# A hybrid decoder layer on one core: feed-forward expansions for all 1024 tokens by seven block products, down products as phases of their own, mixers between them

## The chip, the core and the metric

One core of a Trainium2 chip runs the kernel. The metric is the device time of one execution in microseconds (us). Engines are named as in the profile: PE is TensorE, which multiplies; PEld is its load of the stationary operand; DVE is VectorE, ACT is ScalarE, POOL is GpSimd, SP is SyncE, which here only issues DMAs. Each engine works through a queue of its own, in the order in which the built program holds it.

## What is computed

One decoder layer on x of 1024 tokens by 1024 channels, in float32:

```
x = x + 0.5 * swiglu(rms_norm(x, g1), wg1, wu1, wd1)        # D_FF = 2816
h = rms_norm(x, g2);  q, k, v, qi, ki, wi, u = split(h @ w_in)
score = sum over 4 heads of wi * relu(qi . ki), causal       # indexer
attn  = softmax attention, 8 heads x 64, each query over its 256 best-scored keys
pooled = multiscale_pool(u) @ pool_w * pool_scale
x = x + concat(attn, pooled) @ w_out
x = x + 0.5 * swiglu(rms_norm(x, g3), wg2, wu2, wd2)
swiglu(x, wg, wu, wd) = (silu(x @ wg) * (x @ wu)) @ wd
```

## The kernel before

**Arithmetic.** Every large operand is kept as a sum of two parts, `hi` and `lo`. `mm3` (lines 64 to 67) makes each 128-deep product from three matmuls: hi times hi, hi times lo, lo times hi. Weights come from HBM whole; `weight` (lines 161 to 174) loads a block of 128 x 512 into a buffer `r` (or `br` for the mixers), ACT casts it to the hi part (line 171) and DVE or POOL subtracts to get the lo part (line 172).

**Feed-forward.** `ffn` takes one half of the tokens (512) at a time. For each of 22 blocks of 128 hidden columns it makes the gate and the up product, 8 blocks of depth each (`expand`), and `act` (lines 198 to 205) makes the activation in SBUF. Four such blocks form a group; `down` multiplies a group into the residual, and each partial sum is added from its PSUM bank by DVE (line 220). The four banks' worth of accumulators are named `fg`, and only the feed-forward uses them.

**Mixer.** `mixer(h)` does one half: norm, indexer projection with rotary tables, indexer scores, pooling mixer, projections of v, k and q, then `top_masks`, `attention` and `out_proj`. `top_masks` finds each query's 256th best score bit by bit: 31 steps, each a count on ACT (line 445, Sign with an accumulator) and one on DVE (line 429) of the scores above a trial threshold, followed by four small instructions on DVE (lines 444, 448, 450, 451). A step needs the one before. Two blocks of 128 queries go in one run of 31 steps; half 0 has one run, half 1 has two. Mixers use the banks `ba`, `bt` and `pv` and weight buffers `br`, `bw` of their own.

**Order.** The program is written in the order ffn(0), mixer(0), ffn(1), mixer(1), second ffn(0), second ffn(1). A scheduler at build time then moves instructions within each engine's queue, in so far as buffers and data allow; splits and evacuations of the feed-forward carry a high priority. Since the feed-forward of one half needs nothing from the mixer of the other half, and has buffers of its own, its matmuls stand among those of the mixers.

Of the kernel before, what the change touches and what calls it, by code (L numbers as in the profile page):

```python
# [32 lines left out]
HIGH = 10_000_000  # L33


@with_exitstack
def hybrid_layer(ctx: ExitStack, tc: tile.TileContext, x, ffn1_norm, ffn1_w_gate, ffn1_w_up,
# [23 lines left out]
    def mm(o, lhs, rhs, start, stop):  # L61
        nc.tensor.matmul(o, lhs, rhs, start=start, stop=stop)  # L62
# [26 lines left out]
    x_dr = [dr.tile([HALF, D], F32, name=f"x_dr{h}") for h in range(2)]  # L89

# [9 lines left out]
    def load_x(h):  # L100
        new_x(h)
        for i in range(4):
            r0 = h * HALF + i * 128
            nc.sync.dma_start(x_at(h, i), x[0, r0:r0 + 128, :])
# [32 lines left out]
    def norm_transposed(h, which, region):  # L137
        hT = [t(f"X{region}{j}", [128, 4, HALF], F32R) for j in range(4)]
        xn = []
        for i in range(4):  # L140
            xi = t("sc", [128, D])
            ss = t("st", [128, 8])
            nc.scalar.activation(xi, x_at(h, i), AF.Square, accum_out=ss[:, :1])
            r = rstd_of(ss[:, :1], 1, D)
            nc.vector.tensor_scalar(xi, x_at(h, i), r[:, :1], None, op0=ALU.mult)
            xn.append(xi)
        for k in range(NK):
            ps = bank(("ba", "bt")[k % 2])
# [9 lines left out]
    nsplit = [0]  # L158
    alone = [True]

    def weight(src, tags=("r", "w")):
        """Both parts of a block of weights, [128, 2, a, b] for a source [128, a, b] of at most 512 columns."""
        _, a, b = src.shape
        n = a * b
        nsplit[0] += 1
        raw = t(tags[0], [128, 512])
        nc.sync.dma_start(raw[:, :n].rearrange("p (a b) -> p a b", a=a), src)
        w = t(tags[1], [128, 2, 512], F32R)
        eng = nc.vector if alone[0] or nsplit[0] % 3 == 0 else nc.gpsimd
        with tc.high_priority(offset=HIGH):  # L170
            nc.scalar.copy(w[:, 0, :n], raw[:, :n])  # L171
            eng.tensor_sub(w[:, 1, :n], raw[:, :n], f(w[:, 0, :n]))  # L172
        return w[:, :, :n].rearrange("p l (a b) -> p l a b", a=a)
# [4 lines left out]
    MIX = ("br", "bw")  # L178

# [1 line left out]
    def ffn(h, hT, wg, wu, wd, f0, f1, done=None):  # L181
        hi, lo = hT
        groups = []
        i = f0
        while i < f1:
            n = 4 if f1 - i >= 4 else 2
            groups.append(range(i, i + n))
            i += n
        def expand(ff, w):
            ps = bank("fg")  # L190
            for k0 in range(0, NK, 4):
                wt = weight(rows(w, k0, k0 + 4, ff * 128, (ff + 1) * 128))
                for k in range(k0, k0 + 4):
                    mm3(ps, wt[:, 0, k - k0], wt[:, 1, k - k0], hi[k], lo[k], k == 0, k == NK - 1)
            return ps

        def act(pg, pu):
            with tc.high_priority(offset=HIGH):
                s = t("t", [128, 512])
                nc.scalar.activation(s, pg, AF.Silu)  # L200
                nc.vector.tensor_mul(s, s, pu)  # L201
                a = t("a", [128, 2, 512], F32R)
                nc.scalar.copy(a[:, 0], s)  # L203
                (nc.vector if alone[0] else nc.gpsimd).tensor_sub(a[:, 1], s, f(a[:, 0]))  # L204
            return a

        def down(gr, acts):
            n = len(gr)
            for c in range(2):
                cols = slice(c * 512, (c + 1) * 512)  # L210
                wts = [weight(rows(wd, k, k + 1, c * 512, (c + 1) * 512)) for k in gr]
                for i in range(4):
                    ps = bank("fg")
                    tok = slice(i * 128, (i + 1) * 128)
                    for j in range(n):
                        mm3(ps, acts[j][:, 0, tok], acts[j][:, 1, tok], wts[j][:, 0, 0], wts[j][:, 1, 0],
                            j == 0, j == n - 1)
                    xo = x_at(h, i)[:, cols]
                    with tc.high_priority(offset=HIGH):
                        nc.vector.scalar_tensor_tensor(xo, ps, 0.5, xo, op0=ALU.mult, op1=ALU.add)  # L220
                    if done is not None and gr[-1] == NF - 1:
                        r0 = h * HALF + i * 128
                        nc.sync.dma_start(done[0, r0:r0 + 128, cols], xo)

        pend = None
        for gr in groups:
            acts = []
            for ff in gr:
                pg = expand(ff, wg)
                if pend is not None:  # L230
                    down(*pend)
                    pend = None
                acts.append(act(pg, expand(ff, wu)))
            pend = (gr, acts)
        down(*pend)

# [1 line left out]
    def out_proj(h, region):  # L238
        fetch_x(h)
        mt = [None] * 4  # L240
        for j in (2, 3, 0, 1):
            mt[j] = t(f"X{region}{j}", [128, 2, 2, HALF], F32R)
            nc.gpsimd.dma_start(mt[j].rearrange("p k l c -> p k (l c)"),
                                m_dr[h][2 * j:2 * j + 2].rearrange("k p l c -> p k (l c)"))
        for c in range(2):
            banks = [bank(n) for n in ("ba", "ba", "bt", "bt")]
            for n, k in enumerate((4, 5, 6, 7, 0, 1, 2, 3)):
                wt = weight(rows(w_out, k, k + 1, c * 512, (c + 1) * 512), MIX)
                m = mt[k // 2][:, k % 2]
                for i in range(4):  # L250
                    tok = slice(i * 128, (i + 1) * 128)
                    mm3(banks[i], m[:, 0, tok], m[:, 1, tok], wt[:, 0, 0], wt[:, 1, 0], n == 0, n == NK - 1)
# [5 lines left out]
    def proj(hT, c0, n):  # L258
        hi, lo = hT
        banks = [bank(n) for n in ("ba", "ba", "bt", "bt")]  # L260
        for k in range(NK):
            wt = weight(rows(w_in, k, k + 1, c0, c0 + n), MIX)
            for i in range(4):
                tok = slice(i * 128, (i + 1) * 128)
                mm3(banks[i][:, :n], hi[k][:, tok], lo[k][:, tok], wt[:, 0, 0], wt[:, 1, 0], k == 0, k == NK - 1)
        return banks

    def rope_tables(h):
        cs = t("cs", [128, 4, 2, HD])
# [3 lines left out]
    def index_proj(h, hT, cs):  # L273
        banks = proj(hT, C_I, N_I)
        for i in range(4):
# [18 lines left out]
            ps = bank("pv")  # L294
# [12 lines left out]
    def qk_proj(h, hT, cs, which):  # L307
        banks = proj(hT, (C_Q, C_K)[which], 512)
        for i in range(4):
# [17 lines left out]
            pt = bank("pv")  # L327
# [12 lines left out]
    def v_proj(h, hT):  # L340
        banks = proj(hT, C_V, 512)
# [7 lines left out]
    def pool_mixer(h, hT):  # L349
        hi, lo = hT  # L350
        tiles = []
        for g in range(4):
            ps = bank("bt")
            for kk in range(2):
                wt = weight(rows(w_in, 4 * kk, 4 * kk + 4, C_U + g * 128, C_U + (g + 1) * 128), MIX)
# [7 lines left out]
            po = bank("pv")  # L363
# [29 lines left out]
    def scores(h, i, sc):  # L393
        g = 4 * h + i
        n2 = (g // 2 + 1) * 256
        qi = t("qm", [128, 4, 256], F32R)
        for l in range(2):
            nc.gpsimd.dma_start(qi[l * 64:(l + 1) * 64], qi_dr[h][i].rearrange("h d l c -> d h (l c)"))
        for c0 in range(0, n2, 512):
            cw = min(512, n2 - c0)  # L400
            o = sc[:, c0:c0 + cw]
            for hd in range(4):
                b = bank("ba")
# [12 lines left out]
    def top_masks(h, tiles, sc, masks):  # L416
        """Adds nothing to a query's 256 highest scores (the lowest keys among equal ones), NEG to the others.

        The 256th highest score is built bit by bit from counts; a row's threshold is kept negated,
        with its bits flipped where it is below zero, so that a higher bit pattern is a higher score.  # L420
        """
        m = len(tiles)
        ns = [(4 * h + i + 1) * 128 for i in tiles]
        st = t("sel", [128, 8, 2], I32)
# [11 lines left out]
        for j in range(m):  # L436
            count(j, ALU.is_ge, 0.0)
            nc.vector.memset(goal[:, j:j + 1], float(TOPK) if j else float(2 * TOPK - ns[j]))
# [4 lines left out]
        for bit in range(30, -1, -1):  # L443
            nc.vector.tensor_scalar(v1, v, 1 << bit, None, op0=ALU.bitwise_xor)  # L444
            nc.scalar.activation(masks[0][:, :ns[0]], sc[0][:, :ns[0]], AF.Sign, bias=f(v1[:, 0:1]),  # L445
                                 accum_out=cnt[:, 0:1])
            if m > 1:
                nc.vector.tensor_scalar(th[:, 1:2], f(v1[:, 1:2]), -1.0, None, op0=ALU.mult)  # L448
                count(1, ALU.is_ge, th[:, 1:2])
# [12 lines left out]
        for j in range(m):  # L462
            n, n2 = ns[j], (ns[j] + 255) // 256 * 256
            e, k, s = t("el", [128, S], BF16)[:, :n], masks[j][:, :n], sc[j][:, :n]
# [15 lines left out]
    def attention(h, masks, region):  # L480
# [175 lines left out]
```

## Time and profile before

| | |
|---|---|
| three runs | 1986.48, 1988.6, 1990.12 us, median 1988.6 |
| span of the profiled execution | 1985.0 us, 3.6 us under the median of the runs |
| busy | PE 1936.2, PEld 1592.5, DVE 1115.9, ACT 835.3, POOL 555.2 us |
| PE instructions | 8904 |
| granted clock of PE, mean | 0.995 |
| HBM read, written | 208.45 MB, 31.46 MB |

The span runs from the first to the last instruction; the rest of a run's time lies around it, and no other time of the profiled execution is given. A matmul's duration in the rows overlaps with that of its neighbours, so the pace of PE is read as matmuls per stretch of time. Granted clock 1.00 is the upper of PE's two levels, 2.4 GHz; 0.50 would be the lower, 1.2 GHz.

### The profile page before, as it was taken

The page shows a single profiled execution, that of the slowest core. Times are in us where ns is not written, and L with a number is a line of the kernel's source. Part 1 is how long each engine was busy: PE and PEld are TensorE (multiplying, and loading weights), DVE is VectorE, ACT ScalarE, POOL GpSimd, SP SyncE. Part 2 cuts the span into 40 slices and gives each one's busy share as a digit, 9 for nine tenths or more (in the row PEclk, how much of TensorE's full clock was granted, in tenths as well). Part 3 has the DMA queues.
Part 4 walks back from the last instruction along what each step waited for, and adds up shares of the span by engine and source line. Part 5 has one row for each costly group of instructions (what it writes and reads, how often), then busy time and mean ns, then how long its engine had stood idle before and what let it go on. Part 6 is the DMA issues. An engine that isn't in the chain of part 4 may idle for free.

```text
span 1985.0 us, 25600 instructions
## 1 busy us (share of the span) xinstructions
PE 1936.2 (98%) x8904; PEld 1592.5 (80%) x8904; DVE 1115.9 (56%) x2242; ACT 835.3 (42%) x1550; POOL 555.2 (28%) x550
## 2 busy tenths in 40 slices
PE   7999999999999999999999998999999999999999
PEld 6888888888778888888888777678888878888887
DVE  5434433535985686242447999966767433444344
ACT  5323223344443566232443565437575332322231
POOL 2000000134448643344443343774332210000000
PEclk9999999999999999999999999999999999999999
DMA  7223323434365666333453225485653613333232
GB/s 210 88 89 101 96 90 97 137 110 128 100 167 154 174 157 198 130 91 97 135 137 97 78 93 149 136 199 128 131 140 113 201 42 96 102 95 96 91 106 90
DMA packets 304273, 241.59 MB, mean 122 GB/s; under 512 B 35472, under 2 KB 254736, under 8 KB 304144
## 3 DMA queue, kind: packets, MB, share of 16 engines
q1 hardware_dynamic: 285520, 207.45, 35.2%
q0 software_dynamic: 18624, 32.51, 7.6%
q8 instruction: 70, 1.15, 0.2%
q14 instruction: 59, 0.48, 0.1%
HBM read 208.45 MB, written 31.46 MB: 121 GB/s over the span
## 4 chain that ended last, share of the span: by engine, by line
PE 79%; DVE 13%; issue 3%; POOL 1%; ACT 1%; DMA 1%; SPq 0%; DVEq 0%; POOLq 0%; ACTq 0%
PE fg L62 63%; PE ba L62 6%; PE bt L62 5%; DVE x L429 4%; PE pv L62 2%; PE bt L533 2%; DVE sel L451 1%; DVE sel L450 1%; DVE sel L444 1%; DVE w L172 1%; DVE x L220 1%; POOL st L134 1%; PE ba L150 1%; DMA r<-in_ffn_w_gate_dram 0%; DVE sel L448 0%
## 5 line engine op out<-in xcount | busy, mean ns | idle before, releaser
L171 ACT CAST w<-r 128x512 fp32r<-128x512 f32 x528 | 325.5, 619 | 588.7 <-PE fg L62 304.0
L62 PE MATMUL fg<-XA,w 128*128 128x512 f32 x2112 | 519.6, 398 | 0.2
L62 PE MATMUL fg<-w,a 128*128 128x512 f32 x2112 | 505.4, 393 | 3.5 <-DVE x L220 2.3
L62 PE MATMUL fg<-XB,w 128*128 128x512 f32 x2112 | 497.5, 392 | 0.1
L62 PEld LDWEIGHTS fg<-XA,w 128*128 128x128 f32 x2112 | 394.8, 189 | 90.4 <-ACT XA L153 0.5
L62 PEld LDWEIGHTS fg<-w,a 128*128 128x128 f32 x2112 | 394.0, 188 | 87.5 <-DVE x L220 4.8
L62 PEld LDWEIGHTS fg<-XB,w 128*128 128x128 f32 x2112 | 395.4, 189 | 82.0 <-ACT XB L153 0.5
L172 DVE TENSOR_TENSOR w<-r,w 128x512 fp32r<-128x512 f32 x352 | 255.1, 727 | 317.0 <-ACT w L171 315.2
L172 POOL TENSOR_TENSOR w<-r,w 128x512 fp32r<-128x512 f32 x176 | 234.2, 1335 | 709.2 <-ACT w L171 357.0
L220 DVE SCALAR_TENSOR_TENSOR x<-fg,x 128x512 f32<-128x512 f32 x192 | 129.9, 686 | 122.0 <-PE fg L62 121.6
L172 POOL TENSOR_TENSOR bw<-br,bw 128x512 fp32r<-128x512 f32 (+1 forms) x75 | 95.1, 1273 | 154.8 <-ACT bw L171 146.8
L201 DVE TENSOR_TENSOR t<-t,fg 128x512 f32<-128x512 f32 x88 | 60.2, 684 | 106.4 <-PE fg L62 102.5
L171 ACT CAST bw<-br 128x512 fp32r<-128x512 f32 (+1 forms) x112 | 65.9, 596 | 119.9 <-PE bt L62 101.0
L200 ACT ACTIVATE t<-fg 128x512 f32<-128x512 f32 x88 | 52.4, 596 | 98.1 <-PE fg L62 97.7
L62 PE MATMUL ba<-bw,XB 128*128 128x512 f32 (+1 forms) x288 | 74.7, 384 | 7.1 <-DVE bw L172 2.7
L62 PE MATMUL ba<-bw,XA 128*128 128x512 f32 (+1 forms) x288 | 75.4, 386 | 2.1 <-ACT bw L171 2.1
L172 DVE TENSOR_TENSOR bw<-br,bw 128x512 fp32r<-128x512 f32 (+1 forms) x37 | 27.2, 736 | 86.8 <-ACT bw L171 86.4
L62 PE MATMUL bt<-bw,XB 128*128 128x512 f32 (+1 forms) x288 | 73.5, 382 | 1.6 <-ACT sc L365 1.3
L62 PE MATMUL bt<-bw,XA 128*128 128x512 f32 (+1 forms) x288 | 73.4, 382 | 0.2 <-DVE sel L448 0.2
L445 ACT ACTIVATE x<-sc,sel 128x384 bf16<-128x384 f32 (+1 forms) x62 | 44.6, 719 | 58.9 <-DVE sel L444 57.7
L204 POOL TENSOR_TENSOR a<-t,a 128x512 fp32r<-128x512 f32 x44 | 59.3, 1348 | 35.0 <-ACT a L203 34.6
L62 PEld LDWEIGHTS ba<-bw,XB 128*128 128x128 f32 x288 | 52.1, 189 | 20.2 <-DVE bw L172 3.9
(179 smaller groups left out, 1964.5 us busy)
## 6 DMA issues: line engine op xcount, KB each, us to landing
r<-in_ffn_w_gate_dram SPq DMA_DIRECT2D x176, 256.0 KB, 3.1
r<-in_ffn_w_up_dram SPq DMA_DIRECT2D x176, 256.0 KB, 3.0
r<-in_ffn_w_down_dram SPq DMA_DIRECT2D x176, 256.0 KB, 2.7
br<-in_w_in_dram SPq DMA_DIRECT2D x64, 256.0 KB, 2.7
br<-in_w_out_dram SPq DMA_DIRECT2D x32, 256.0 KB, 3.0
qm<-q_dr POOLq DMA_DIRECT2D x32, 256.0 KB, 4.1
x<-in_x_dram SPq DMA_DIRECT2D x8, 512.0 KB, 7.0
x_dr<-x SPq DMA_DIRECT2D x4, 1024.0 KB, 4.7
```

The source lines that it names most:

```text
L62: nc.tensor.matmul(o, lhs, rhs, start=start, stop=stop)
L134: nc.gpsimd.tensor_tensor(r[:, :n], r[:, :n], mhalf[:, :n], op=ALU.pow)
L150: nc.tensor.transpose(ps[:, i * 128:(i + 1) * 128], xn[i][:, k * 128:(k + 1) * 128], ident)
L171: nc.scalar.copy(w[:, 0, :n], raw[:, :n])
L172: eng.tensor_sub(w[:, 1, :n], raw[:, :n], f(w[:, 0, :n]))
L200: nc.scalar.activation(s, pg, AF.Silu)
L201: nc.vector.tensor_mul(s, s, pu)
L204: (nc.vector if alone[0] else nc.gpsimd).tensor_sub(a[:, 1], s, f(a[:, 0]))
L220: nc.vector.scalar_tensor_tensor(xo, ps, 0.5, xo, op0=ALU.mult, op1=ALU.add)
L429: nc.vector.tensor_scalar(masks[j][:, :ns[j]], sc[j][:, :ns[j]], thr, None, op0=op, op1=ALU.add, accum_out=cnt[:, j:j + 1])
L445: nc.scalar.activation(masks[0][:, :ns[0]], sc[0][:, :ns[0]], AF.Sign, bias=f(v1[:, 0:1]), accum_out=cnt[:, 0:1])
L533: nc.tensor.transpose(tp[:, j * 128:(j + 1) * 128], sm[ti][:, (2 * k2 + kk) * 128:(2 * k2 + kk + 1) * 128], ident)
```

## The change

**Expansions.** All 1024 tokens at once. `norm_blocks` transposes the normalised x into four blocks (two halves of depth by two halves of tokens) and forms from them the seven operands of Strassen's method in Winograd's form, each split into hi and lo. `quad` does the same to a 1024 x 256 piece of weights: POOL makes four sums and differences, ACT casts seven operands and DVE subtracts seven. `product` multiplies a pair: 4 blocks of depth, 12 matmuls. Seven products replace eight, and DVE and ACT combine them in SBUF on the way out. The activations go to DRAM (`a_dr`).

**Down products.** `down` is a phase of its own: it reads activations and weights back as pieces of 128 x 512, splits both, and sums all 22 depth blocks in four banks.

**Mixers.** Split weights for the mixers are made during the first expansion (`make_piece`) and stored in DRAM, 512 KB each; the mixers load them already split. The program order changes, `top_masks` takes all four blocks of half 1 in one run, and pools of buffers and banks are shared by all parts.

```diff
-    BUFS = {"r": 3, "w": 6, "a": 4, "t": 2, "br": 3, "bw": 3, "sc": 4, "mk": 4, "qm": 2,
-            "st": 4, "cs": 1, "sel": 2, "x8": 4}
-    PBUFS = {"fg": 3, "ba": 2, "bt": 2, "pv": 1}
+    BUFS = {"X": 14, "x8": 4, "w": 7, "sc": 4, "mk": 6, "st": 4, "sel": 1, "pw": 1, "st2": 1}
+    PBUFS = {"fg": 4, "m": 4}
...
+    def piece(src, eng, tag="w"):
+        n = int(np.prod(src.shape[1:]))
+        raw = t("mk", [128, 512])
+        nc.sync.dma_start(raw[:, :n] if len(src.shape) == 2 else
+                          raw[:, :n].rearrange("p (a b) -> p a b", a=src.shape[1]), src)
+        w = t(tag, [128, 2, 512], F32R)
+        with tc.high_priority(offset=HIGH):
+            split(w[:, 0, :n], w[:, 1, :n], raw[:, :n], eng)
+        return w
...
+    def make_piece():
+        i, src = next(pieces, (None, None))
+        if src is not None:
+            n = src.shape[1] * src.shape[2]
+            w = piece(src, nc.gpsimd, "sc")
+            nc.sync.dma_start(p_dr[i][:, :, :n], f(w[:, :, :n]))
+
+    def get_piece(i, n=512):
+        w = t("w", [128, 2, 512], F32R)
+        nc.sync.dma_start(f(w[:, :, :n]), p_dr[i][:, :, :n])
+        return w[:, :, :n]
...
+    def norm_blocks(which):
+        B = {p: (t("X", [128, 4, HALF], F32R), t("X", [128, 4, HALF], F32R)) for p in "1267543"}
+        xn = {(h, i): normed(h, i, "w" if h else "sc") for h in range(2) for i in range(4)}
...
+        for k in range(4):
+            s = t("x8", [128, 4, 512])
...
+            for p in "167543":
+                split(B[p][0][:, k], B[p][1][:, k], src[p], nc.vector if p in "165" else nc.gpsimd)
+        return B
+
+    def quad(W, j):
+        raw = t("x8", [128, NK, 256])
+        for k in range(0, NK, 4):
+            nc.sync.dma_start(raw[:, k:k + 4], rows(W, k, k + 4, 256 * j, 256 * j + 256))
+        s = t("x8", [128, 4, 4, 128])
...
+            for p in "1675243":
+                out[p] = t("w", [128, 2, 4, 128], F32R)
+                split(out[p][:, 0], out[p][:, 1], src[p], nc.vector)
+        return out
+
+    def product(o, w, b, first):
+        for k in range(4):
+            mm(o, w[:, 0, k], b[0][:, k], first and k == 0, False, not first)
+            mm(o, w[:, 0, k], b[1][:, k], False, False, not first)
+            mm(o, w[:, 1, k], b[0][:, k], False, k == 3, not first)
...
+    def down(h, a_in, wd, tags, eng, done=None):
+        for c in range(2):
+            cols = slice(c * 512, (c + 1) * 512)
+            banks = [bank(tags[c]) for _ in range(4)]
+            for k in range(NF):
+                at = piece(a_in[k, :, h * HALF:(h + 1) * HALF], eng())
+                wt = piece(rows(wd, k, k + 1, c * 512, (c + 1) * 512), eng())
                 for i in range(4):
...
+                    mm3(banks[i], at[:, 0, tok], at[:, 1, tok], wt[:, 0], wt[:, 1], k == 0, k == NF - 1)
...
-    hT0 = norm_transposed(0, 0, "A")
-    ffn(0, hT0, *w1, 0, 4)
...
-    mixer(0, "A")
-    hT0 = norm_transposed(0, 2, "A")
-    ffn(1, hT1, *w1, 0, NF)
-    mixer(1, "B")
...
+    B = norm_blocks(0)
+    expand(B, ffn1_w_gate, ffn1_w_up, a_dr[0], make_piece)
+    load_x(0)
+    down(0, a_dr[0], ffn1_w_down, ("fg", "m"), vector_most)
+    hT0, cs0, masks0, top0 = mixer_front(0)
+    load_x(1)
+    top_masks(*top0)
+    down(1, a_dr[0], ffn1_w_down, ("fg", "fg"), pool_most)
+    mixer_proj(0, hT0, cs0)
+    hT1, cs1, masks1, top1 = mixer_front(1)
+    top_masks(*top1)
+    attention(0, masks0)
+    mixer_proj(1, hT1, cs1)
+    out_proj(0)
+    park_x(0)
+    attention(1, masks1)
+    out_proj(1)
+    park_x(1)
+    B = norm_blocks(2)
+    expand(B, ffn2_w_gate, ffn2_w_up, a_dr[1])
+    fetch_x(0)
+    down(0, a_dr[1], ffn2_w_down, ("fg", "m"), vector_most, out)
+    fetch_x(1)
+    down(1, a_dr[1], ffn2_w_down, ("fg", "m"), vector_most, out)
```

`mixer_front` is norm, indexer projection and scores; `mixer_proj` is v, k, q and the pooling mixer. The built queues show where the work of these calls stands. In the queue of ACT before, during the 31 steps of half 0's masks (L445), casts of feed-forward weights (`w<-r`) and mixer weights (`bw<-br`) stand between the steps:

```order
L445 ACTIVATE x_3121,sel_4072<-sc_3122,sel_4072 128x384
L171 CAST w_5847<-r_5845 128x512
L171 CAST w_5852<-r_5850 128x512
L171 CAST w_5914<-r_5912 128x512
L445 ACTIVATE x_3121,sel_4072<-sc_3122,sel_4072 128x384 x2
L171 CAST bw_3439<-br_3437 128x512
L445 ACTIVATE x_3121,sel_4072<-sc_3122,sel_4072 128x384 x2
```

In the queue of ACT with the change, at the same masks (L555 now), after the indexer scores (L518) and ahead of the first casts of half 1's down product (L164):

```order
L518 ACTIVATE mk_4975<-m_4972 128x512
L518 ACTIVATE mk_4981<-m_4978 128x512
L555 ACTIVATE x_4930,sel_4993<-sc_4931,sel_4993 128x384 x31
L164 CAST w_5218<-mk_5216 128x512
L164 CAST w_5223<-mk_5221 128x512
```

All 31 steps now stand in one piece, and every cast of that down product behind them.

In the queue of ACT with the change, at the masks of half 1, where exponentials (L628) and copies (L648) of half 0's attention stand between the first five steps only; a step is a pair of L555 rows:

```order
L628 ACTIVATE sc_8075,st_8074<-sc_8075,st_8074 128x512
L628 ACTIVATE sc_8085,st_8084<-sc_8085,st_8084 128x512
L628 ACTIVATE sc_8133,st_8132<-sc_8133,st_8132 128x256
L628 ACTIVATE sc_8143,st_8142<-sc_8143,st_8142 128x256
L555 ACTIVATE x_7284,sel_7479<-x_7285,sel_7479 128x640
L555 ACTIVATE x_7284,sel_7479<-x_7286,sel_7479 128x1024
L555 ACTIVATE x_7284,sel_7479<-x_7285,sel_7479 128x640
L555 ACTIVATE x_7284,sel_7479<-x_7286,sel_7479 128x1024
```

From there 26 pairs follow each other with nothing between, and the rest of half 0's attention comes behind them.

In the queue of PE before, in the attention of half 1 (scores `ba<-XB,qm`, values `pv`), expansions of the second feed-forward of half 0 (`fg<-XA,w`) stand between its parts:

```order
L62 MATMUL fg_13342<-XA_5332,w_13345 128x512
L62 MATMUL ba_10435<-XB_10341,qm_10348 128x512 x2
L62 MATMUL ba_10439<-XB_10341,qm_10348 128x256
L62 MATMUL pv_10381<-XB_9766,x_10029 128x256
L62 MATMUL ba_10439<-XB_10341,qm_10348 128x256
L62 MATMUL fg_13342<-XA_5332,w_13345 128x512
L62 MATMUL pv_10381<-XB_9766,x_10029 128x256 x7
```

With the change, at the start of that attention, the last matmuls of half 0's output projection (`m<-w,X`) are followed by scores (`m<-X,w`) and transposes (L644) alone:

```order
L62 MATMUL m_9444<-w_9544,X_9320 128x512 x3
L62 MATMUL m_9445<-w_9544,X_9320 128x512 x3
L62 MATMUL m_9577<-X_9565,w_9572 128x512 x2
L62 MATMUL m_9581<-X_9565,w_9572 128x256 x2
L62 MATMUL m_9592<-X_9565,w_9572 128x512 x2
```

From here to its end no feed-forward matmul stands in PE's queue.

## Rows read from the trace of the kernel before

**Rows 1.** The page, busy time of each engine.
```profile
PE 1936.2 (98%) x8904; PEld 1592.5 (80%) x8904; DVE 1115.9 (56%) x2242; ACT 835.3 (42%) x1550; POOL 555.2 (28%) x550
```
**Rows 2.** The page, chain that ended last, by engine.
```profile
PE 79%; DVE 13%; issue 3%; POOL 1%; ACT 1%; DMA 1%; SPq 0%; DVEq 0%; POOLq 0%; ACTq 0%
```
**Rows 3.** Busy time by stretch: from:to, length, engines (instructions), granted clock, DMA share, GB/s.
```profile
1100.00:1200.00 100.00, 90.71 (x377) 70.47 (x376) 99.05 (x271) 62.11 (x130) 41.95 (x41) 0.98 0.30 92
1800.00:1900.00 100.00, 100.00 (x443) 82.84 (x442) 42.09 (x62) 29.05 (x48) 0.00 (x0) 1.00 0.33 98
```
**Rows 4.** Groups by form: line, engine, operation, tiles, count, busy us, mean ns, idle before.
```profile
L62 PE MATMUL fg<-XA,w 128*128 128x512 f32 x2112 | 519.6, 398 | 0.2
L171 ACT CAST w<-r 128x512 fp32r<-128x512 f32 x528 | 325.5, 619 | 588.7 <-PE fg L62 304.0 <-issue 145.1 <-DMA r<-in_ffn_w_up_dram 86.9
L172 DVE TENSOR_TENSOR w<-r,w 128x512 fp32r<-128x512 f32 x352 | 255.1, 727 | 317.0 <-ACT w L171 315.2
L172 POOL TENSOR_TENSOR w<-r,w 128x512 fp32r<-128x512 f32 x176 | 234.2, 1335 | 709.2 <-ACT w L171 357.0 <-DVE t L201 342.9 <-issue 8.9
L220 DVE SCALAR_TENSOR_TENSOR x<-fg,x 128x512 f32<-128x512 f32 x192 | 129.9, 686 | 122.0 <-PE fg L62 121.6
```
**Rows 5.** Timeline of the start: start us, length, engine, line, tiles, idle before.
```profile
4.21 1.06 ACT L143 ACTIVATE sc<-x 128x1024 f32<-128x1024 f32 x1 [2.20 <-DMA x<-in_x_dram]
...
9.23 1.06 ACT L143 ACTIVATE sc<-x 128x1024 f32<-128x1024 f32 x1 [0.20 <-DMA x<-in_x_dram]
...
15.86 1.22 PE L62 MATMUL fg<-XA,w 128*128 128x512 f32 x2
```
**Rows 6.** Groups by form: squares and scaled copies of the norms on ACT.
```profile
L143 ACT ACTIVATE sc<-x 128x1024 f32<-128x1024 f32 x24 | 25.3, 1054 | 15.8 <-DVE x L255 8.5 <-DMA x<-in_x_dram 3.8 <-DVE x L220 3.6
L153 ACT ACTIVATE XB<-bt,gains 128x512 fp32r<-128x512 f32 x12 | 8.3, 688 | 11.3 <-PE bt L150 11.3
```
**Rows 7.** DMA issues: tiles, queue, count, KB each, median us from issue to landing.
```profile
x<-in_x_dram SPq DMA_DIRECT2D x8, 512.0 KB, 7.0
...
m_dr<-mk SPq DMA_DIRECT2D x16, 256.0 KB, 6.0
...
XB<-m_dr POOLq DMA_DIRECT2D x4, 1024.0 KB, 8.1
...
qm<-qi_dr POOLq DMA_DIRECT2D x12, 256.0 KB, 4.0
...
qi_dr<-mk SPq DMA_DIRECT2D x8, 256.0 KB, 2.7
```
**Rows 8.** Timeline of DVE in a mask step of half 0 without other work between.
```profile
503.32 0.17 DVE L444 TENSOR_SCALAR sel<-sel 128x2 int32<-128x2 int32 x1
...
504.96 0.17 DVE L444 TENSOR_SCALAR sel<-sel 128x2 int32<-128x2 int32 x1
```
**Rows 9.** Groups by form: counts of the mask steps on DVE and ACT.
```profile
L429 DVE TENSOR_SCALAR_CACHE_REDUCE x<-sc,sel 128x768 bf16<-128x768 f32 x33 | 33.3, 1008 | 0.3
L445 ACT ACTIVATE x<-x,sel 128x896 bf16<-128x896 f32 x31 | 32.4, 1044 | 57.9 <-DVE sel L444 56.7 <-DVE sel L451 1.2
L445 ACT ACTIVATE x<-sc,sel 128x640 bf16<-128x640 f32 x31 | 25.5, 822 | 21.1 <-DVE sel L444 21.0
L429 DVE TENSOR_SCALAR_CACHE_REDUCE x<-x,sel 128x896 bf16<-128x896 f32 x2 | 2.3, 1146 | 0.1
```
**Rows 10.** Groups by form: the largest of attention on DVE.
```profile
L511 DVE CUSTOM_DVE_ANT_0 sc<-ba,x 128x512 f32<-128x512 f32 x64 | 43.1, 685 | 17.9 <-PE bt L533 14.3 <-PE ba L62 3.0
L538 DVE TENSOR_TENSOR XB<-bt,XB 128x512 fp32r<-128x512 f32 x56 | 37.5, 684 | 6.5 <-ACT XB L537 5.9
L519 DVE TENSOR_SCALAR sc<-sc,st 128x1024 f32<-128x1024 f32 x16 | 12.0, 752 | 0.5
```
**Rows 11.** Groups by form: POOL's reciprocal root in the norms of q and k.
```profile
L134 POOL TENSOR_TENSOR st<-st,mhalf 128x8 f32<-128x8 f32 x16 | 29.6, 1853 | 0.3
```
**Rows 12.** Busy time by stretch, at the norm of half 1's second feed-forward.
```profile
1610.00:1620.00 10.00, 5.75 (x23) 4.01 (x24) 6.21 (x10) 5.99 (x12) 4.55 (x8) 0.71 0.01 2
```

More of the change, by code (lines that the diff above doesn't have):

```diff
@@ L33 @@
 HIGH = 10_000_000
+NPIECE = 56
 @with_exitstack
@@ L155, in norm_transposed, with split @@
         return [hT[k // 4][:, k % 4] for k in range(NK)], [hT[2 + k // 4][:, k % 4] for k in range(NK)]
[L158 to L169, printed above, removed]
+    def split(hi, lo, src, eng):
+        nc.scalar.copy(hi, src)
+        eng.tensor_sub(lo, src, f(hi))
@@ new lines, in mixer_pieces @@
+    def mixer_pieces():
+        for which in range(3):
+            for k in range(NK):
+                yield rows(w_in, k, k + 1, (C_Q, C_K, C_V)[which], (C_Q, C_K, C_V)[which] + 512)
+        for k in range(NK):
+            yield rows(w_in, k, k + 1, C_I, C_I + N_I)
+        for g in range(4):
+            for kk in range(2):
+                yield rows(w_in, 4 * kk, 4 * kk + 4, C_U + g * 128, C_U + (g + 1) * 128)
+        for k in range(NK):
+            for c in range(2):
+                yield rows(w_out, k, k + 1, c * 512, (c + 1) * 512)
@@ L218, in down @@
[L218 to L234, printed above, removed]
@@ L235, in ffn, with out_proj @@
-        down(*pend)
-    def out_proj(h, region):
+                    mm3(banks[i], at[:, 0, tok], at[:, 1, tok], wt[:, 0], wt[:, 1], k == 0, k == NF - 1)
+            for i in range(4):
+                xo = x_at(h, i)[:, cols]
+                with tc.high_priority(offset=HIGH):
+                    nc.vector.tensor_add(xo, banks[i], xo)
+                if done is not None:
+                    r0 = h * HALF + i * 128
+                    nc.sync.dma_start(done[0, r0:r0 + 128, cols], xo)
+    def out_proj(h):
@@ L245, in out_proj @@
         for c in range(2):
-            banks = [bank(n) for n in ("ba", "ba", "bt", "bt")]
+            banks = [bank("m" if h == 0 or c else "fg") for _ in range(4)]
             for n, k in enumerate((4, 5, 6, 7, 0, 1, 2, 3)):
-                wt = weight(rows(w_out, k, k + 1, c * 512, (c + 1) * 512), MIX)
+                wt = get_piece(P_O + 2 * k + c)
                 m = mt[k // 2][:, k % 2]
@@ L402, in scores @@
             for hd in range(4):
-                b = bank("ba")
+                b = bank("m")
                 for l in range(2):
@@ L444, in top_masks @@
             nc.vector.tensor_scalar(v1, v, 1 << bit, None, op0=ALU.bitwise_xor)
[L445 to L449, printed above, removed]
+            for j in act:
+                nc.scalar.activation(masks[j][:, :ns[j]], sc[j][:, :ns[j]], AF.Sign, bias=f(v1[:, j:j + 1]),
+                                     accum_out=cnt[:, j:j + 1])
+            nc.vector.tensor_scalar(th[:, dve], f(v1[:, dve]), -1.0, None, op0=ALU.mult)
+            for j in range(m):
+                if j not in act:
+                    count(j, ALU.is_ge, th[:, j:j + 1])
             nc.vector.tensor_tensor(taken, cnt, goal, op=ALU.is_ge)
@@ L579, in mixer, with mixer_proj @@
         todo = [i for i in range(4) if 4 * h + i >= 2]
-        sc = {i: t("sc", [128, S]) for i in todo[:2]}
-        if len(todo) > 2:
-            more = t("x8", [128, 2, S])
-            sc.update({i: more[:, j] for j, i in enumerate(todo[2:])})
+        if h:
+            more = [t("x8", [128, 2, S]) for _ in range(2)]
+            sc = {i: more[n // 2][:, n % 2] for n, i in enumerate(todo)}
+        else:
+            sc = {i: t("sc", [128, S]) for i in todo}
         for i in todo:
             scores(h, i, sc[i])
-        pool_mixer(h, hT)
+        for i in range(4):
+            if i not in todo:
+                causal_mask(i, masks[i])
+        return hT, cs, masks, (h, todo, [sc[i] for i in todo], [masks[i] for i in todo])
+    def mixer_proj(h, hT, cs):
         v_proj(h, hT)
```

239 lines of the change are left out of this document (140 added, 99 removed).

## The prediction

> **What bounds the kernel now.** I read the page first. PE is busy 98% of the span [rows 1] and carries 79% of the chain that ended last, DVE 13% [rows 2]: the kernel is bound by PE almost everywhere, and PE stands idle for only 1985.0 − 1936.2 = 49 us. The stretches tell the pace: where the feed-forward runs alone, 443 matmuls pass in 100 us at clock 1.00, so one costs PE 0.2257 us. Where mixer work is densest, DVE is busy 99 of 100 us and PE still 90.7 [rows 3]. That row is the one to keep in mind: the mixers are work for DVE and ACT, and PE stays busy beside them because feed-forward matmuls stand among theirs in its queue. Where none do, at the norm ahead of the last feed-forward part, PE is busy 57% and its clock falls to 0.71 [rows 12]. So two things decide: how many matmuls are saved, and what covers the mixers afterwards.
>
> **What is removed.** Each feed-forward had 22 × 2 × 8 depth blocks × 3 matmuls for each half, 4224 expansions in all. Seven products of 12 matmuls, for 22 gate or up pieces, twice, are 3696. The other matmuls stay, 2112 of them down products. The saving is 528 × 0.2257 = 119 us of PE. It would be the whole result if PE remained as full as it is.
>
> **What is moved.** The orders above say that it does not. All 31 mask steps of half 0 stand in one piece on ACT ahead of every cast of the down product that was to run beside them, and PE cannot multiply before a cast. For half 1, 26 of 31 pairs stand in one piece. Then mixer_proj(1), out_proj(0) and attention(1) follow with no feed-forward matmul in PE's queue. The cover of [rows 3] is gone, so I add the stages up one behind the other, each by the engine that is slowest in it. Durations are those of the trace, counts those of the built queues.
>
> 1. Start to the first product. Before, the first product began at 15.9, after four squares. 2 MB of x had landed for the one at 9.23 [rows 5]; 4 MB, at the rate from 4.21 to 9.23, for the eighth by about 19. Behind it ACT has some 12 scaled copies at 0.69 and 24 casts at 0.62 before the first operands are whole [rows 4, 6], 23 us, and the first weight piece takes its buffers from the same pools, about 8. With a few waits between engines **52** (44 to 60).
> 2. Expansions: 3696 × 0.2257 = 834. A product of seven lasts 19 us on PE. Its seven subtractions on DVE take 5.1 and its seven casts on ACT 4.3 [rows 4]; five combinations on DVE at about 0.69 make 3.4, four sums on POOL at 1.34 make 5.3. All are covered, as are the six pieces for the mixers per 38 us (POOL 6 × 1.34 = 8). They share buffers with the combinations, for which I add 8. **842** (834 to 874).
> 3. Four down phases: 2112 × 0.2257 = 477, and 4 us for each phase's first pieces (one landing of 256 KB [rows 7]): **493** (477 to 537). Of the 192 additions on DVE at 0.686 [rows 4] only 32 remain; those were hidden, so this removes nothing from the sum.
> 4. Mixer front of half 0: norm 9.5 (four squares and a chain of transposes and copies), indexer projection about 15, then rotary work, a round trip through DRAM (2.7 and 4.0 [rows 7]) and scores, about 22, estimates by queue counts: **46** (36 to 55).
> 5. Masks of half 0: a step takes 1.64 [rows 8], 31 take 51; first bounds 3, and the masks themselves with the queue of casts that must refill behind them 11. **65** (51 to 75), all of it idle on PE.
> 6. Projections of half 0: 384 matmuls, 87. POOL's reciprocal root of 1.85 comes four times per projection [rows 11] between bank and bank; with waits at the three changes of projection and the first landing I add 30. **117** (95 to 140).
> 7. Mixer front of half 1, with twice the keys: **62** (50 to 75).
> 8. Masks of half 1 and attention of half 0. One run now covers four blocks, so a step has two counts on DVE (1.01 and 1.15) and two on ACT beside them [rows 9], and four or five small instructions of about 0.16 each [rows 8]: 3.15. 26 steps make 82. The mixed start is 57, the masks' end 40, the rest of attention 53, by their DVE rows. **232** (200 to 270).
> 9. Projections of half 1 with out_proj(0): 384 + 192 matmuls are 130; with the waits of term 6 **163** (145 to 190).
> 10. Attention of half 1, by DVE: 56 sums 37.5, 48 scores at 0.685 make 32.9, 16 subtractions at 0.75 make 12.0 [rows 10]; the smaller groups bring it to 134. It is a chain of DVE, ACT and PE, so I take 85% for DVE, the largest row being 99% with two halves' work to choose from [rows 3]: **158** (134 to 190).
> 11. out_proj(1): a store and a load of m, 6.0 and 8.1 [rows 7], and 96 matmuls of each column half, the first of which alone waits; 14 + 21 = **35** (28 to 42). The second half's 22 us lies beside the next norm, as squares need x; I count it there.
> 12. Second norm of all tokens: as term 1 without the load, **37** (28 to 45).
> 13. Last sums and stores: **5** (5 to 6).
>
> The sum is 52 + 842 + 493 + 46 + 65 + 117 + 62 + 232 + 163 + 158 + 35 + 37 + 5 = 2307, a span. The profiled execution's span of before was 1985.0, the median of the runs 3.6 more, so **2311 us**, 16% above before. As a cross-check: PE's work falls to about 1936 − 119 = 1817, so the forecast says that PE stands idle for some 490 us against 49.
>
> **A rule and a row.** At the norm where PE is busy 57%, its clock is 0.71, between the two levels [rows 12]. The Trainium skill, "TensorE: Matmul & The Clock Gate", section "Why this matters for your kernels", tells writers to leave no idle gaps of TensorE between bursts of matmuls, as the clock then falls back to its lower level. The trace agrees with that row, and the rule speaks against this change.
>
> **The rivals.** (a) *Faster.* The mixers are covered as the program's order reads: down(1) runs beside the masks, and every mixer stage costs only its PE work. Then the terms outside the mixers stand, 842 + 493 + 52 + 37 + 5 = 1429, with 35 for the output projection's end 1464, and the mixers' matmuls and transposes add some 492 by queue counts: 1956 + 3.6, about 1960, 1.4% faster. For it speaks that before did just this [rows 3]. Against it speaks ACT's order. It decides where less than about 30 us of mixers stay uncovered, and masks alone leave 65 + 82. Chance 0.03.
>
> (b) *Slower clock.* Stages 4 to 11 hold about 490 us of PE work in pieces with gaps. The forecast has it all at 0.2257 a matmul. If an eighth of it runs as at [rows 12] or lower and also lengthens chains, in which a transpose's end is waited for, I estimate 60 us more: about 2375. For it: that row. Against it: attention is bound by DVE, which would hide a part. At the far end half of the 490 would run at half speed and nothing would hide it, 245 more: 2555. DVE and ACT set most of these stages, so I hold that for unlikely. Chance 0.17 for 2375, 0.02 for the far end. The page's rule, taken at its word, would lead to the far end.
>
> (c) *Feed.* A down phase now needs two pieces of 256 KB for every 12 matmuls, 2.71 us, or 193 GB/s, where before 98 were moved in the pure feed-forward [rows 3], through six buffers. A buffer is held from issue to the last split. At a landing of 4.0 [rows 7] plus 2 us of split a pair needs 6 of the 3 × 2.7 = 8.1 us that three pairs of buffers give. At a landing of 7.0, as x had, it needs 9, 11% over: 53 us on 477, and some 25 on the projections, whose pieces of 512 KB are as dense: about 2390. Chance 0.12.
>
> (d) *It is not what the words say:* if the products were not seven, PE would show 4224 expansions; the built queue holds 3696, so nothing is put on this.
>
> **The numbers.** The forecast case has 0.66, with its own range of 2230 to 2390, by the terms' bounds, which do not all fall to one side. The range, 2205 to 2440, takes in the middle of (b) and (c). 0.2% (4 us) is about what a measurement of this kernel can tell from no change. Faster by more has 0.03, the chance of (a); within it 0.01, for a value between (a) and the forecast; slower 0.96.
>
> **What would show it.** In the changed profile PE should be busy about 1820 us of 2310, near 79%. The first expansion should run at 443 matmuls per 100 us, and last about 420 us. Then the down phase at the same pace; then a stretch of 50 us and more in which PE has nothing and ACT and DVE alternate between their counts (L555 on ACT; masks of half 0), and one of 80 us in half 1. In attention of half 1 DVE should be over 80% busy and PE around half. The chain should give DVE and ACT some 20% more than before. If down phases run below 443 matmuls per 100 us with PE waiting for casts or landings, (c) is right; if the granted clock of the mixers' stretches is well below 1.00 and stages are longer with the same order, (b). I am wrong if feed-forward matmuls run during the masks, or if the expansions, which I took as covered, are held up by buffers.

## The result, and the profile after

The median of the runs is 2270.3 us against 1989.3: a ratio of 1.143, interval 1.141 to 1.145, so 281 us slower. The forecast was 2311, its range 2205 to 2440. The profiled execution took 2279.0, 8.7 above the median, with a span of 2277.3; stages are read from it.

The page of the changed kernel: busy time (as [rows 1]), and the span in 40 slices of 57 us, in tenths.

```profile
PE 1912.6 (84%) x8376; PEld 1536.1 (67%) x8376; DVE 1211.7 (53%) x2264; ACT 849.7 (37%) x1596; POOL 748.0 (33%) x673
...
PE   3999999999933999656018978885999999999999
...
DVE  5655665644457112339995326956555555534443
...
PEclk8999999999966999867559989998999999999999
```

528 instructions left PE, and yet only 24 us of its busy time. PE now idles 2277.3 − 1912.6 = 365 us, against 49. The holes are where the forecast put them, in the middle slices: PE shows 3 and 3 in the two with the masks of half 0 (DVE 5 and 7), and 6, 0 and 1 in the three in which DVE shows 9 (masks of half 1).

Busy time by stretch of the changed kernel (columns as [rows 3]): an expansion, a down phase, the masks of half 0, the pooling mixer of half 0, mask steps of half 1, attention of half 1.

```profile
250.00:350.00 100.00, 100.00 (x430) 80.42 (x430) 62.29 (x72) 39.45 (x69) 51.99 (x38) 1.00 0.59 198
...
2100.00:2200.00 100.00, 100.00 (x442) 82.81 (x442) 43.24 (x53) 41.56 (x74) 32.44 (x25) 1.00 0.64 206
...
658.00:714.00 56.00, 0.34 (x1) 0.34 (x2) 47.91 (x198) 23.94 (x67) 0.82 (x1) 0.52 0.05 14
950.00:982.00 32.00, 9.38 (x17) 4.16 (x18) 7.55 (x20) 7.70 (x19) 13.82 (x23) 0.50 0.24 81
1084.00:1171.00 87.00, 0.00 (x0) 0.00 (x0) 80.61 (x229) 51.67 (x101) 0.00 (x0) 0.50 0.00 0
1392.00:1507.00 115.00, 92.39 (x551) 71.81 (x552) 106.95 (x332) 74.31 (x147) 9.86 (x14) 0.97 0.67 160
```

The first two rows have PE full at clock 1.00, but the expansion passes 430 matmuls where the down phase passes 442. Masks leave PE nothing (0.3 of 56, 0 of 87 us); attention of half 1 has DVE at 93%.

The timeline of PE at the masks of half 0, and that of DVE in two mask steps of half 1:

```profile
656.78 1.10 PE L62 MATMUL m<-ki,w 128*128 128x512 f32 x4
713.66 1.65 PE L62 MATMUL fg<-w,w 128*128 128x512 f32 x3 [55.79 <-ACT w L164]
```
```profile
1120.30 0.17 DVE L553 TENSOR_SCALAR sel<-sel 128x4 int32<-128x4 int32 x1
...
1123.33 0.17 DVE L553 TENSOR_SCALAR sel<-sel 128x4 int32<-128x4 int32 x1
1123.53 0.17 DVE L557 TENSOR_SCALAR sel<-sel 128x2 f32<-128x2 f32 x1
1123.73 1.01 DVE L538 TENSOR_SCALAR_CACHE_REDUCE x<-x,sel 128x768 bf16<-128x768 f32 x1
1124.67 0.08 DVE L538 DVE_READ_ACCUMULATOR x<-x,sel 128x1 f32 x1
1124.67 1.14 DVE L538 TENSOR_SCALAR_CACHE_REDUCE x<-x,sel 128x896 bf16<-128x896 f32 x1
1125.74 0.08 DVE L538 DVE_READ_ACCUMULATOR x<-x,sel 128x1 f32 x1
1125.92 0.16 DVE L561 TENSOR_TENSOR sel<-sel 128x4 int32<-128x4 f32 x1
1126.12 0.17 DVE L562 COPY_PREDICATED sel<-sel 128x4 int32<-128x4 int32 x1
1126.32 0.17 DVE L553 TENSOR_SCALAR sel<-sel 128x4 int32<-128x4 int32 x1
```

PE waits 55.8 us for the cast that stands behind the 31st step on ACT. A step of four blocks takes 3.0 us.

The terms of the forecast beside the stages, bounded by PE's matmuls (timeline of PE) so that they add up to the span. Terms 1, 5 and 12 end where the next stage's matmuls begin, the others with their own last. Where two stages overlap, term 8 ends at 1220.3, as the projections of half 1 begin, although the last matmuls of half 0's attention come 11 us later; term 10 ends at 1517.8, although out_proj(1) begins at 1506.7.

| term | forecast | measured |
|---|---|---|
| 1 start to first product | 52 | 44.5 |
| 2 two expansions | 842 | 884.7 |
| 3 four down phases | 493 | 497.5 |
| 4 front of half 0 | 46 | 48.1 |
| 5 masks of half 0 | 65 | 55.8 |
| 6 projections of half 0 | 117 | 137.0 |
| 7 front of half 1 | 62 | 60.7 |
| 8 masks of half 1, attention of half 0 | 232 | 177.4 |
| 9 projections of half 1, out_proj(0) | 163 | 169.2 |
| 10 attention of half 1 | 158 | 128.3 |
| 11 out_proj(1) | 35 | 39.3 |
| 12 second norm | 37 | 30.7 |
| 13 end | 5 | 4.1 |
| span | 2307 | 2277.3 |

### The profile page after: what moved, and what is told of

Same layout as the page of the kernel before. It is cut to its first block, busy times and chain, and to the rows that moved or that the text cites. A ratio compares the mean times of both kernels' runs of the same rounds, so it can differ in the third digit from the quotient of the medians.

```text
span 2277.3 us, 25227 instructions
## 1 busy us (share of the span) xinstructions
PE 1912.6 (84%) x8376; PEld 1536.1 (67%) x8376; DVE 1211.7 (53%) x2264; ACT 849.7 (37%) x1596; POOL 748.0 (33%) x673
## 5 line engine op out<-in xcount | busy, mean ns | idle before, releaser
L62 PE MATMUL m<-X,w 128*128 128x512 f32 (+1 forms) x2232 | 544.4, 398 | 20.1 <-DVE X L649 7.4
L62 PEld LDWEIGHTS m<-X,w 128*128 128x128 f32 x2232 | 418.4, 191 | 119.0 <-DVE st L622 8.8
L62 PE MATMUL fg<-X,w 128*128 128x512 f32 x1848 | 446.6, 401 | 48.8 <-ACT w L164 46.6
L62 PEld LDWEIGHTS fg<-X,w 128*128 128x128 f32 x1848 | 352.4, 191 | 137.5 <-ACT w L164 48.2
L165 DVE TENSOR_TENSOR w<-x,w 128x512 fp32r<-128x512 f32 x308 | 274.8, 896 | 176.2 <-ACT w L164 172.8
L62 PE MATMUL fg<-w,w 128*128 128x512 f32 x1320 | 307.7, 395 | 66.4 <-ACT w L164 60.4
L164 ACT CAST w<-x 128x512 fp32r<-128x512 f32 x308 | 190.1, 620 | 403.4 <-PE m L62 216.8
L165 POOL TENSOR_TENSOR w<-mk,w 128x512 fp32r<-128x512 f32 x154 | 200.9, 1312 | 406.9 <-ACT w L164 353.3
L62 PEld LDWEIGHTS fg<-w,w 128*128 128x128 f32 x1320 | 251.5, 191 | 122.5 <-ACT w L164 62.4
L164 ACT CAST w<-mk 128x512 fp32r<-128x512 f32 x352 | 203.9, 619 | 304.9 <-PE fg L62 96.1
L62 PE MATMUL m<-w,X 128*128 128x512 f32 (+1 forms) x1056 | 244.7, 391 | 14.7 <-DMA w<-p_dr 6.6
L62 PE MATMUL fg<-X,X 128*128 128x256 f32 x320 | 71.6, 331 | 114.1 <-DVE mk L659 88.9
```

Of the source, the lines that this page charges most:

```text
L62: nc.tensor.matmul(o, lhs, rhs, start=start, stop=stop, skip_group_check=goes_on)
L164: nc.scalar.copy(hi, src)
L165: eng.tensor_sub(lo, src, f(hi))
```

## The experiments

Two questions were open: whether the place of the masks in the queues is what costs, and why the expansions, with PE full, ran at 0.2333 us a matmul. The second came first. The kernel before was run again beside the experiments, with medians of 1987.8 to 1988.9; the changed kernel was not, so its 2270.3 (2269.5 to 2279.0) is the one that every difference below is taken from.

The trace of before has the same two paces: where its feed-forward reads XA, 434 matmuls pass in 100 us, not the 443 of [rows 3], which is a stretch that reads XB.

```profile
100.00:200.00 100.00, 100.00 (x434) 81.23 (x433) 39.60 (x59) 30.11 (x50) 0.00 (x0) 1.00 0.31 95
```

What sets X and XA apart is where the build lays them: it gives tiles places in the order of their first use, so small tiles made earlier move large ones. A matmul has two such operands, the stationary one, whose load is PEld, and the moving one. In the expansions w is the stationary one and X the moving one.

**X moved (e1), and the kernel before with XA moved (e3).** The same line, added behind `load_gains()`:

```diff
     load_gains()
+    nc.vector.memset(t("st", [128, 8]), 0.0)
```


> The changed kernel with the small tiles st made first, which moves the 14 tiles X, sc and mk up by 128 bytes in each partition (X from byte 0xdaa0 to 0xdb20) and leaves w where it was (0x30b20); nothing else changes. In the trace of the changed kernel every matmul that reads an X tile follows the one before it by 0.233 us, every one that reads two w tiles by 0.227, at granted clock 1.00; in the kernel before, those that read XA (0xdaa0) took 0.2325 and those that read XB (0x26320) 0.2276. Theory A, the place in SBUF sets the pace: expansions come to 0.227 us a matmul, 3696 x 0.0065 = 24 us, and the projections give some 5 more; 2270 falls to about 2242 (2235 to 2250). Theory B, the pace comes from what runs beside the expansions (transfers, DVE, POOL): no change, 2266 to 2274.

> The kernel before, with st made first, so that XA moves from byte 0xdaa0 to 0xdb20 and XB stays at 0x26320. Theory A: the some 2400 matmuls that read XA go from 0.2325 to 0.2276 us, 12 us less, and since PE bounds that kernel all of it shows: about 1977 (1974 to 1982). Theory B: 1989, no change.

e1 took 2251.1 us, 19 less than the changed kernel, where theory A gave 28 and 2235 to 2250. The profiled spans differ by 34, as the changed kernel's was its slowest execution and e1's its fastest; PE's busy time in them fell by 29. Why the median fell by less is open. e3 took 1977.1 against 1988.7, a ratio of 0.9943 (0.9929 to 0.9956), as theory A gave. In e1's trace both expansions pass 443 matmuls in 100 us (first row), and in e3's so does the stretch beside XA that passed 434 before (second row):

```profile
250.00:350.00 100.00, 100.00 (x443) 82.81 (x442) 62.86 (x72) 40.50 (x70) 52.00 (x38) 1.00 0.57 191
...
100.00:200.00 100.00, 100.00 (x443) 82.81 (x442) 41.56 (x61) 31.26 (x52) 0.00 (x0) 1.00 0.33 97
```

DVE, ACT, POOL and the transfers are as busy in e1's stretch as in the slow one of the changed kernel, so theory B falls.

**X and w moved (e2), w alone (e5).** In `norm_blocks`, behind the tiles X; e2 has the line of e1 too:

```diff
+        if which == 0:
+            nc.vector.memset(t("sel", [128, 8, 4]), 0.0)
         xn = {(h, i): normed(h, i, "w" if h else "sc") for h in range(2) for i in range(4)}
```


> As the last one, X at 0xdb20, and w moved by 128 bytes as well, from 0x30b20 to 0x30ba0, so that now w stands where X stood, modulo 256 bytes. Theory A, if either operand in such a place slows a matmul: expansions stay at 0.233 and down products, which read w twice, go from 0.227 to 0.233, 2112 x 0.0065 = 14 us more than the changed kernel, about 2284. Theory A, if only the moving operand counts: expansions (moving X) gain 24 us, down products and projections (moving w) lose 14 and 5, about 2262. Theory B: 2270, all unchanged.

> The changed kernel with w moved up by 128 bytes (0x30b20 to 0x30ba0) and X left at 0xdaa0, so that both now begin at 0xa0 modulo 256. Theory A2, formed on the last two runs: a matmul takes 0.233 us when its two operands begin 128 bytes apart modulo 256, and 0.227 when they begin alike, wherever that is; then all matmuls of X and w come to 0.227, and the time to that of the run with X moved, 2251 (2240 to 2256). Rival A1, the place 0xa0 itself is slow for the operand X: 0.233 stays, 2270.

e2 took 2275.3 us, within the spread of the changed kernel's runs. Neither option of theory A held: expansions stayed slow, and down phases, with both operands in the place that had looked slow, stayed fast. That is the "all unchanged" of theory B, which e1 and e3 had ruled out (e2, an expansion and a down phase):

```profile
250.00:350.00 100.00, 100.00 (x432) 81.10 (x431) 60.27 (x71) 38.66 (x68) 51.54 (x38) 1.00 0.57 194
...
2100.00:2200.00 100.00, 100.00 (x443) 82.81 (x442) 44.15 (x53) 41.62 (x74) 32.04 (x25) 1.00 0.63 203
```

A reading that fits all three runs is that no place is slow by itself, but the two operands' places against each other matter. e5 tests this: X where it was, w moved to begin alike modulo 256. It took 2248.9 us, 21 less, as A2 gave and not A1, and its expansions pass 443:

```profile
250.00:350.00 100.00, 100.00 (x443) 82.81 (x442) 62.22 (x71) 39.83 (x70) 51.19 (x38) 1.00 0.57 192
```

**32 and 64 bytes apart (e9, e10).** As e1, with the small tiles `mhalf` (e9), and `mhalf` and `pscale` (e10), made behind X and kept in a list `mh`:

```diff
-    mhalf = sb.tile([128, 8], F32, name="mhalf")
...
+        if which == 0:
+            mh.append(sb.tile([128, 8], F32, name="mhalf"))
```


> The changed kernel with X at byte 0xdb00 and w at 0x30b20, 32 bytes apart modulo 256 (by where small tiles are placed; nothing else). Theory A2 was seen at 0 (0.227 us a matmul) and 128 (0.233) alone. If any difference costs, expansions show 0.233 here; if only a half of 256 bytes does, 0.227; a value between would show that the cost grows with the difference.

> The changed kernel with X at byte 0xdae0 and w at 0x30b20, 64 bytes apart modulo 256 (by where small tiles are placed, and the small constants loaded after the first norm). As in the last run: 0.233 if any difference costs, 0.227 if only 128 does, a value between if it grows.

One run each, 2276.0 us both, within the spread of the changed kernel's runs. The expansions of either (e9 here) pass 430:

```profile
250.00:350.00 100.00, 100.00 (x430) 80.58 (x429) 56.90 (x70) 38.68 (x68) 52.21 (x38) 1.00 0.56 193
```

Of the four differences tried, 32, 64 and 128 cost the expansions the same, 0 nothing; others were not tried.

**The down product ahead of the masks of half 0 (e4).**

```diff
-    top_masks(*top0)
     down(1, a_dr[0], ffn1_w_down, ("fg", "fg"), pool_most)
+    top_masks(*top0)
```


> The changed kernel with two lines exchanged: the down product of half 1 stands ahead of the masks of half 0 in the program, so that in the queue of ACT casts of that down product now stand between the mask steps, one to three steps at a time. Theory of the prediction, PE's idle time at these masks is the price of their place in the queues: the 56 us without matmuls at half 0's masks go, and the down product pays a little for DVE and ACT work between its splits; about 2217 (2205 to 2235). Rival, the down product and the masks want the same ACT and DVE, so that one delays the other by what is gained: 2255 or more.

2237.8 us: 33 less, not 56 and not none; the theory's range ended at 2235, the rival's began at 2255. Busy time of e4 in the down phase with the masks beside it, a piece of its PE timeline, and what ACT does before the last of these rows:

```profile
659.00:806.00 147.00, 130.49 (x532) 100.74 (x533) 107.86 (x251) 68.63 (x148) 85.75 (x65) 0.97 0.53 166
```
```profile
681.04 1.21 PE L62 MATMUL fg<-w,w 128*128 128x512 f32 x4 [0.40 <-ACT w L164]
682.41 7.74 PE L62 MATMUL fg<-w,w 128*128 128x512 f32 x32 [0.15 <-POOL w L165]
691.51 3.02 PE L62 MATMUL fg<-w,w 128*128 128x512 f32 x12 [1.36 <-ACT w L164]
694.94 1.19 PE L62 MATMUL fg<-w,w 128*128 128x512 f32 x4 [0.41 <-ACT w L164]
```
```profile
693.67 0.62 ACT L555 ACTIVATE x<-sc,sel 128x384 bf16<-128x384 f32 x1 [1.69 <-DVE sel L553]
...
694.29 1.12 ACT L164 CAST w<-mk 128x512 fp32r<-128x512 f32 x2
```

The 55.8 us hole is gone. The 528 matmuls take 147 us, against some 120 where a down phase runs alone: a cast (L164) now stands on ACT behind a mask step's count (L555, Sign) whose threshold comes from DVE, and PE waits a little at every few casts. The theory holds for the larger part, the rival for the rest.

**Masks of half 1 in two runs (e7).**

```diff
-    top_masks(*top1)
+    for j in (0, 2):
+        top_masks(top1[0], top1[1][j:j + 2], top1[2][j:j + 2], top1[3][j:j + 2])
```


> The changed kernel with the masks of half 1 in two runs of two blocks each, as in the kernel before, in place of one run of four. Theory, one run of four is a gain, because a step's four small instructions on DVE and the way from ACT to DVE are paid 31 times and not 62: the two runs take some 1.9 + 2.1 us a pair of steps against 3.0, 31 us more less what of half 0's attention fits between, 2290 (2280 to 2305). Rival, a run of two leaves room for attention and the change to four is worth nothing: 2270.

2309.4 us, 39 more: a loss, as the theory said, but past the 31 that it gave before anything fits between, and 4 past its range. The longest stretch without a matmul grows from 88.9 to 137.7 us. Steps of the first run and of the second (DVE):

```profile
1089.92 0.17 DVE L553 TENSOR_SCALAR sel<-sel 128x2 int32<-128x2 int32 x1
1091.84 0.17 DVE L553 TENSOR_SCALAR sel<-sel 128x2 int32<-128x2 int32 x1
...
1150.30 0.17 DVE L553 TENSOR_SCALAR sel<-sel 128x2 int32<-128x2 int32 x1
1152.48 0.17 DVE L553 TENSOR_SCALAR sel<-sel 128x2 int32<-128x2 int32 x1
```

1.9 and 2.2 us, together 4.1 against 3.0. Taking all four blocks in one run is a part of the change that gains.

**Eight products (e6).**

```diff
                 product(b5, w["3"], B["3"], False)
+                product(b5, w["3"], B["3"], False)
```


> The changed kernel with the seventh product of each gate or up piece made twice, so that eight products of 12 matmuls stand where seven did (the doubled one is added twice into its sum, so that the values differ from the layer's); 528 more matmuls, all else as it is. The step of the prediction that the expansions are bound by PE: 528 x 0.2333 = 123 us more than the changed kernel, 2393 (2385 to 2401). Rival, a part of the expansions waits for splits, so that more matmuls fill waiting time: less than 110 us more.

2389.0 us (two runs, 2385.5 and 2392.4), 118.7 more; 528 matmuls at 0.2333 make 123. So the expansions are bound by PE, and 528 matmuls fewer are worth their time in this arrangement too. The other work of seven products, the sums, splits and combinations, is the same in e6; a kernel with eight real products was not run.

**Masks of half 1 beside the projections (e8).** With the edits of e1 and e4:

```diff
-    mixer_proj(0, hT0, cs0)
     hT1, cs1, masks1, top1 = mixer_front(1)
+    mixer_proj(0, hT0, cs0)
+    mixer_proj(1, hT1, cs1)
     top_masks(*top1)
     attention(0, masks0)
-    mixer_proj(1, hT1, cs1)
     out_proj(0)
```


> The changed kernel with X moved as in the first run, the down product of half 1 ahead of the masks of half 0 as in the fourth, and the order of the second half: mixer front of half 1, projections of half 0, projections of half 1, and then its masks and the attention of half 0, so that mask steps of half 1 stand between the projections' instructions in the queues. Theory of the prediction, masks cost what they stand alone: the first two give 19 and 32, the 75 us of 25 steps of half 1 without matmuls go, of which the fourth run lets expect some six tenths to all: about 2150 (2115 to 2180). Rival, attention of half 0, which had mask steps to share its time with, takes by itself what is saved: 2215 or more. By no theory does it come near the kernel before, as both attentions stay without feed-forward matmuls beside them.

2145.9 us, 124 less than the changed kernel. Less e1's 19 and e4's 33, 73 are left for this order, if the three add up; it was not run alone. The 88.9 us without a matmul are gone: from 650 to 1240 us PE's longest wait is 11.6. Busy time of e8 in a stretch with mask steps of half 1 among projections, PE at 80% and DVE at 91%:

```profile
850.00:1000.00 150.00, 119.30 (x483) 93.44 (x484) 136.37 (x346) 79.55 (x159) 41.66 (x55) 0.88 0.56 173
```

It is still 8.0% slower than the kernel before (7.8 to 8.1). Of all versions only e3, the kernel before with XA moved, is faster than the kernel before.

## Why the prediction was right, and where its terms were off

**What was right.** The mechanism: 119 us of matmuls are saved, and more than that is lost because masks and attention stand in the queues where no feed-forward matmul is beside them. e6 confirms that the saving is real; that its 118.7 us meets 119 so closely is chance, as 123 was expected of it. Rival (a), faster, fell as the order of ACT's queue said it would: the 55.8 us hole ends with the cast behind the 31st step.

**What is shown, and what is read from rows.** For the masks e4 and e8 show the cause by moving it: the same work costs 33 and some 73 us less in other places of the queues, with no instruction of it taken away. That is 106 of some 400 us lost (281 and the 119 saved). e1's placing gives 19 more. For the rest, attention, the norms, the start and the pooling mixer, no run moves the work. That it costs so much for want of matmuls beside it is argued from rows: in e8 PE still idles 262 us (2143.1 − 1881.4), against 49 before.

**The sum was better than its terms.** Taken without sign the thirteen terms miss by 189 us together, their sum by 30. That they cancel so far is luck.

**Term 2, 43 us too small.** The step that failed is "3696 × 0.2257 = 834". The pace came from one stretch of [rows 3], in which the moving operand was XB. The row at 100 to 200 us of the same trace shows the slower pace beside XA; I had not read it. At the measured pace 3696 × 0.2333 = 862, 28 more; the other 22, for which I had 8, are the first pieces of each expansion (9.5 and 7.9 us more than their matmuls need before the products run on, at a mean granted clock of 0.64) and the turns between phases. The covers I named held: with e1's placing an expansion runs at 443 with all splits and all mixer pieces beside it.

**Terms 8 and 10, 55 and 30 us too large.** Term 8 had four parts. The mixed start took 38 us (57 in the forecast), the 26 steps 78 (82, as a step takes 3.0 and not 3.15), the masks' end until PE's next matmul 12 (40), the rest 49 (53). The masks' end and attention, which I had one behind the other, overlap. For term 10 the 85% was near the truth; the 134 us of DVE were not. In attention of half 1:

```profile
1389.50:1517.80 128.30, 105.69 (x617) 82.73 (x617) 112.10 (x344) 76.11 (x150) 11.04 (x16) 0.97 0.62 150
```

DVE is busy 112.1 of 128.3 us, 87% (93% without the two ends). The durations of these instructions add up to 132.6, about what I had, but durations in DVE's rows overlap: in the mask steps above, a count of 1.01 us starts at 1123.73 and the next at 1124.67, 0.94 later. Durations added up gave too much work for the same reason in the mixed start, 49 us where DVE is busy 38.

**Term 6, 20 too small.** The waits at the changes of projection are 2.1 and 2.4 us, shorter than I had. What I had not priced is the pooling mixer: from 945 to 982 PE has little but a chain of DVE, POOL and ACT to wait for, 9.4 us of work in 32 in the row above. The other terms were within 10 us. The errors above add to −55 − 30 + 43 + 20 = −22, most of the 30 by which the span came out shorter.

**The cross-check** had PE's work at 1817 and its idle time at 490; they are 1912.6 and 365. The slower pace is one part of the 96 us of work that are too many: e1, which removes it, has 1883.2. The clock is likely another. Eleven of the 46 stretches of 50 us have a granted clock under 0.9; their busy time multiplied by what is missing to 1.00 makes 63 us. This is an estimate, and rather too high, as a stretch's mean clock takes in its idle time. A matmul that stands alone also counts with its whole duration, 0.4 us in [rows 4], so the two parts cannot be told apart sharply.

**Rival (b)** was true of the clock, 0.50 to 0.52 in the masks and in the pooling mixer, but the total did not come near its 2375. In the masks there is hardly a matmul to slow: 0.3 of 56 us and 0 of 87. In the pooling mixer there are 9.4 us of PE's work, in chains that wait for it. The Trainium skill, "TensorE: Matmul & The Clock Gate", section "Why this matters for your kernels", tells writers to leave no such gaps; the trace agrees that the clock falls in them, and shows that the total stayed below the forecast nonetheless. No run separated what the lower clock cost in the stages that PE shares.

**Rival (c)**, the feed, did not come: the down phases pass 442 matmuls in 100 us, at 206 GB/s.

**Signs that did not come.** PE was to be busy near 79% and is at 84%, for the reasons above. In attention of half 1 it was to be around half and is at 80% (92.4 of 115 us). The chain was to give DVE and ACT some 20% more; on the page it gives them 3% and 1%, but it reaches back no further than 1293 us, behind both masks, so it says nothing of them.

## What to carry to other kernels

Before work is taken away from a full engine, look in the built queues for what its matmuls were covering: here 119 us fewer matmuls cost 281, since steps that only DVE and ACT work on lost their cover, and moving the masks gave some 106 of it back. Where an engine sets a stage's time, take its busy time from a stretch and not from durations added up: in attention of half 1 DVE's were 112 and 133 us. And read a pace for each pair of operands, not once for a kernel: two stretches with the same instruction, both full and at clock 1.00, differed by 3%.

## What had not been expected of the hardware

A matmul of 128 x 512 in float32r follows the last after 0.227 us where its two operands begin at the same byte modulo 256 in their partitions, and after 0.233 where they begin 128 bytes apart, or, in the expansions, 32 or 64. The projections, in which X is stationary and w moves, show it too. The first 192 matmuls of half 0's projections (timeline of PE) in the changed kernel (128 apart), in e1 (alike), in e10 (64 apart) and in e9 (32 apart):

```profile
845.19 44.79 PE L62 MATMUL m<-w,X 128*128 128x512 f32 x192
```
```profile
830.74 43.68 PE L62 MATMUL m<-w,X 128*128 128x512 f32 x192
```
```profile
844.71 44.11 PE L62 MATMUL m<-w,X 128*128 128x512 f32 x192
```
```profile
844.85 44.95 PE L62 MATMUL m<-w,X 128*128 128x512 f32 x192
```

That is 0.233, 0.228, 0.230 and 0.234 us, so with these roles exchanged 64 bytes cost less than 128 and 32 do not. That 256 is the period rests on three distances from X to w: 0x23000 bytes in e1 and 0x23100 in e5 are fast, 0x23080 in the changed kernel is slow. Nine pairs of places were seen (XA and XB against w before, which begins at byte 32 modulo 256 there, X against w in the changed kernel, e1, e2, e5, e9 and e10, XA in e3): the four alike modulo 256 are all fast, the five others all slower. 128 bytes of placing were worth 0.6% of the kernel before. Why, the traces do not show.
